# An encoder block on one core: q and k of three heads ahead of every v and gate, all v and gates as groups of seven products

## The chip, the cores and the metric

The kernel runs on one core of a Trainium2 chip. The metric is the device time of one execution in microseconds (us); less is better. Engines are called PE (TensorE: matmuls), DVE (VectorE), ACT (ScalarE), POOL (GpSimd) and SP (SyncE, which issues most transfers).

## The reference

One layer on x of 512 tokens and 1024 features, all in float32. Cut to what the change touches:

```python
h = rmsnorm(x, g_mix)
xc, gb, gc, q, k, v, g_sw, gate_a, gate_r = split(h @ w_in)   # 1024 x5, 2048 x2, 1024 x2 columns
# 4 heads: q, k of 256 columns, v of 512
q, k = rotary(q) * 256 ** -0.5, rotary(k)
ret = forward retention (gamma_f, with the diagonal) + backward retention (gamma_b, strictly future)
y_r = (groupnorm(ret) * silu(g_sw)) @ w_r_out
y_a = (gb * conv3(gc * xc)) @ w_a_out
x = x + (sigmoid(gate_a) * y_a + sigmoid(gate_r) * y_r) @ w_o
x = x + (silu(rms(x) @ w_gate) * (rms(x) @ w_up)) @ w_down
y = rmsnorm(x, g_final)
```

Retention of a head is (q k^T * decay) v, where the decay of a pair of tokens is gamma to the power of their distance.

## The kernel before, in words

Each float32 matrix is split into two parts: `split` rounds it (`hi`, an ACT copy) and takes the rest (`lo`, a DVE difference), and `mm3` does three matmuls for one product (hi hi, hi lo, lo hi). Weights stream from memory in the order of a list, `plan()`: SP loads raw pieces into 10 buffers (`raw`), ACT and DVE split them into 5 units (`whi`, `wlo`), PE uses them in order. The raw loads run four items of the list ahead, the splits two units.

The list has two kinds of items. A chunk is a plain block of weights. A quad is a group of seven products in place of eight (Strassen's way): for four blocks of weights, b11 to b22, DVE adds raw pieces (L244) to make the weight sums t1 to t4, and x has its own sums s1 to s4 (`sums`). `strassen` runs the seven products of 24 matmuls into PSUM and forms the four results with ACT copies (`snap`) and DVE additions (L390, L395, L402).

The beginning goes so:

- SP loads weights, the gains `cols` and x in turn, in pieces of 256 KB (`prefetch_block`, `load_x`). x with its gain is split into `xu`; the row sums of squares (`SumSq`) give 1/rms: `rstd_tokens` lets PE add over the features, takes the power on POOL and writes a diagonal; `rstd_row` lets PE spread it into a row over all partitions (L493, L494).
- v and the swish gate of head 0 are two plain products from `xu` (`token_major`); ACT multiplies the result by 1/rms on its way out of PSUM. Meanwhile DVE multiplies x by the row and splits it again, into `xg`, and makes the sums of x.
- From then on: q and k of head 0 from `xg` (`do_qk`), then for each further head a quad of v and gate and `do_qk`; then two quads of the branch gates. `do_qk` is two chunks of 48 matmuls; DVE rotates the results straight out of PSUM (L619 to L621) and `keep` splits and stores them to memory.
- The decay tables of the four heads (`decays`) need the logarithm of gamma, a series in small DVE steps (`lw`, `lgam`, L506 to L525). A table is one exponential over 896 columns; its store is on SP's queue.

Later stages (gated convolution, scores, outputs, feed-forward) are not touched, but for the last two products: `ev` calls `to_y` (add, square and sum), `put` for the block before (scale and store) and `rms`.

A scheduler sets the order on each engine from the written order, the dependencies and its own model of durations; each engine then works strictly in its order. Short-lived tiles (`t512`) rotate through 9 buffers, large ones (`big`) through 14.

Of the kernel before, what the change touches and what calls it, by code (L numbers as in the profile page):

```python
# [46 lines left out]


# [7 lines left out]
def plan():  # L56
# [86 lines left out]
def block_kernel(ctx: ExitStack, tc: tile.TileContext, xT, xtok, wpack, wquad, cols, decs, rot, g_ffn, g_final, out):  # L143
# [24 lines left out]
    def split(src, hi, lo, scale=None):  # L168

        if scale is None:  # L170
            nc.scalar.copy(hi, src)  # L171
            nc.vector.tensor_tensor(out=lo, in0=src, in1=hi.bitcast(F32), op=ALU.subtract)  # L172
        else:
            nc.scalar.activation(hi, src, AF.Copy, scale=scale)  # L174
            nc.vector.scalar_tensor_tensor(  # L175
                out=lo, in0=src, scalar=scale, in1=hi.bitcast(F32),
                op0=ALU.mult, op1=ALU.subtract)

# [10 lines left out]
    block = [0]  # L189
    ready = []  # L190
# [9 lines left out]
    def prefetch_block(pieces, loads, splits, inbig):  # L200
# [6 lines left out]
        for c in range(2 * per):  # L207
            nc.sync.dma_start(st[c // per][:, c % per * m:(c % per + 1) * m], wpack[i][:, c * m:(c + 1) * m])
            if loads:
                loads(c)  # L210
        for half in range(2):
            hi, lo = unit(inbig)
            units.append((hi, lo))
            for c in range(per):
                sl = slice(c * m, (c + 1) * m)
                split(st[half][:, sl], hi[:, sl], lo[:, sl])
# [191 lines left out]

    ones = const.tile([P, P], F32, name="ones")
# [6 lines left out]
    cols_sb = const.tile([P, N_COLS], F32, name="cols_sb")  # L416
# [12 lines left out]
    def load_x(k, n=1):  # L429
        if k == 0:  # L430
            nc.sync.dma_start(cols_sb, cols)
        nc.sync.dma_start(xs[k // 4][:, k % 4:k % 4 + n, :], xT[:, k:k + n, :])
# [11 lines left out]
    prefetch(2)  # L444
# [6 lines left out]
    class SumSq:  # L451
# [18 lines left out]
        def rstd_tokens(self):  # L470
# [17 lines left out]
            return r  # L488
# [9 lines left out]
    for k in range(8):  # L498
        ss.add(xs[k // 4][:, k % 4, :])
    ss.split()  # L500

# [25 lines left out]

    def decays():
        delta_i = big.tile([P, 896], mybir.dt.int32, tag="big", name="delta_i", padded_shape=[P, 2048])
        nc.gpsimd.iota(delta_i, pattern=[[1, 896]], base=-384, channel_multiplier=-1)  # L530
        delta = big.tile([P, 896], F32, tag="big", name="delta", padded_shape=[P, 2048])
        nc.vector.tensor_copy(delta, delta_i)
        for h in range(HEADS):
            scr = big.tile([P, 896], F32, tag="big", name="scr", padded_shape=[P, 2048])
            tab = misctile(896, "tab")
# [681 lines left out]
```

## Time and profile before

| | |
|---|---|
| Runs | 1043.32, 1044.6, 1044.88 us; median 1044.6 |
| Profiled execution | 1043.97 us, span 1042.2 us |
| PE | 1028.3 us busy |
| DVE, ACT, POOL | 875.5, 523.4, 107.7 us busy |
| From memory, to memory | 135.56 MB, 38.54 MB |
| Granted PE clock | 0.998 |

A row of the timeline is: start in us, duration, engine, line of the kernel, operation, output<-input, shapes, count, and in brackets how long the engine stood before and for whom. A row of the list of waits is: who waited <- for whom: us in total, times, longest. A row of the chain of work is: start, duration, what. Matmuls overlap, so the pace is read from the starts.

### The profile page before, as it was taken

To read this page: it belongs to the slowest core of one execution; us is meant where nothing else is said; L and a number is where in the kernel's file an instruction comes from. 1 tells how busy PE (TensorE), PEld (TensorE's weight loads), DVE (VectorE), ACT (ScalarE), POOL (GpSimd) and SP (SyncE) were. 2 spreads that over 40 slices of the span, in tenths; PEclk is the share of its full clock that TensorE was granted. 3 is DMA by queue.
4 is the path that set the end of the run, shared out by engine and by line. 5 is a ranking of instruction groups with operands and counts; after the bars stand their busy time and mean duration, and the time that the engine had idled before them with its cause. 6 is when DMAs were issued, how large, how long until landed. Compare 5 with 4: busy or idle time off the path is not lost.

```text
span 1042.2 us, 14832 instructions
## 1 busy us (share of the span) xinstructions
PE 1028.3 (99%) x5664; PEld 897.0 (86%) x5664; DVE 875.5 (84%) x1127; ACT 523.4 (50%) x698; POOL 107.7 (10%) x180
## 2 busy tenths in 40 slices
PE   8999999999999999999999999999999999999996
PEld 7788888888888998888888888889998999899985
DVE  6999786858787888697989998669998899889995
ACT  6546745452656545243443234355555565556553
POOL 0121111111111004202011000000002000110011
PEclk9999999999999999999999999999999999999999
DMA  9635638173645576919176535630319322663322
GB/s 325 223 117 201 236 123 281 71 254 119 199 141 182 169 284 233 341 42 358 42 283 247 205 111 173 236 113 28 92 45 275 117 85 78 193 152 102 122 35 87
DMA packets 49688, 175.07 MB, mean 168 GB/s; under 512 B 6480, under 2 KB 6480, under 8 KB 46288
## 3 DMA queue, kind: packets, MB, share of 16 engines
q1 hardware_dynamic: 36592, 131.12, 36.9%
q0 software_dynamic: 13024, 43.00, 12.9%
q8 instruction: 44, 0.72, 0.3%
q14 instruction: 28, 0.23, 0.1%
HBM read 135.56 MB, written 38.54 MB: 167 GB/s over the span
## 4 chain that ended last, share of the span: by engine, by line
PE 77%; issue 9%; DVE 7%; DMA 3%; POOL 2%; ACT 1%; SPq 0%; POOLq 0%; DVEq 0%; ACTq 0%
PE bank L369 29%; PE bank L325 27%; PE bank L285 7%; PE bank L284 7%; PE bank L286 7%; DVE wlo L172 1%; POOL z L566 1%; DVE big L185 1%; DMA big<-ql 1%; DMA big<-xT 1%; DMA z<-t 1%; DMA tab<-tab 0%; DVE big L172 0%; DVE t L464 0%; DVE big L175 0%
## 5 line engine op out<-in xcount | busy, mean ns | idle before, releaser
L171 ACT CAST whi<-raw 128x1024 fp32r<-128x1024 f32 (+1 forms) x281 | 288.6, 1032 | 302.7 <-PE bank L369 66.4
L172 DVE TENSOR_TENSOR wlo<-raw,whi 128x1024 fp32r<-128x1024 f32 (+1 forms) x281 | 335.8, 1202 | 108.8 <-ACT whi L171 107.8
L325 PE MATMUL bank<-xform,whi 128*128 128x256 f32 x1440 | 260.3, 283 | 0.0
L325 PEld LDWEIGHTS bank<-xform,whi 128*128 128x128 f32 x1440 | 224.8, 192 | 0.7 <-ACT t L376 0.6
L325 PE MATMUL bank<-xform,wlo 128*128 128x256 f32 x720 | 203.7, 283 | 0.0
L369 PE MATMUL bank<-whi,big 128*128 128x512 f32 x548 | 172.4, 390 | 0.0
L244 DVE TENSOR_TENSOR raw<-raw 128x1024 f32<-128x1024 f32 (+1 forms) x124 | 148.5, 1205 | 1.8 <-DMA raw<-wquad 0.4
L325 PEld LDWEIGHTS bank<-xform,wlo 128*128 128x128 f32 x720 | 138.2, 192 | 0.0
L369 PEld LDWEIGHTS bank<-whi,big 128*128 128x128 f32 x548 | 102.7, 188 | 22.4 <-DVE big L172 0.6
L369 PE MATMUL bank<-wlo,big 128*128 128x512 f32 x274 | 106.7, 389 | 0.0
L369 PE MATMUL bank<-whi,xform 128*128 128x512 f32 x320 | 101.2, 389 | 0.3 <-ACT t L376 0.3
L284 PE MATMUL bank<-whi,big 128*128 128x512 f32 x240 | 94.3, 395 | 1.8 <-ACT big L174 1.8
L285 PE MATMUL bank<-wlo,big 128*128 128x512 f32 x240 | 94.3, 393 | 0.0
L286 PE MATMUL bank<-whi,big 128*128 128x512 f32 x240 | 93.4, 392 | 0.0
L284 PE MATMUL bank<-big,whi 128*128 128x512 f32 x224 | 87.1, 389 | 0.0
L285 PE MATMUL bank<-big,whi 128*128 128x512 f32 x224 | 87.1, 389 | 0.0
L286 PE MATMUL bank<-big,wlo 128*128 128x512 f32 x224 | 87.1, 389 | 0.0
L376 ACT COPY t<-bank 128x512 f32<-128x512 f32 x96 | 55.5, 585 | 35.8 <-PE bank L369 17.2
L369 PEld LDWEIGHTS bank<-whi,xform 128*128 128x128 f32 x320 | 60.1, 188 | 13.1 <-ACT t L376 0.7
L369 PE MATMUL bank<-wlo,xform 128*128 128x512 f32 x160 | 62.2, 389 | 0.0
L369 PEld LDWEIGHTS bank<-wlo,big 128*128 128x128 f32 x274 | 51.4, 188 | 10.5
L284 PEld LDWEIGHTS bank<-whi,big 128*128 128x128 f32 x240 | 45.5, 190 | 12.5 <-ACT big L174 2.1
(173 smaller groups left out, 1398.6 us busy)
## 6 DMA issues: line engine op xcount, KB each, us to landing
raw<-wquad SPq DMA_DIRECT2D x124, 512.0 KB, 4.4
raw<-wpack SPq DMA_DIRECT2D x58, 512.0 KB, 4.9
z<-t POOLq DMA_DIRECT2D x24, 256.0 KB, 4.9
zform<-z POOLq DMA_DIRECT2D x6, 1024.0 KB, 6.2
v<-t POOLq DMA_DIRECT2D x16, 256.0 KB, 5.0
sg<-t POOLq DMA_DIRECT2D x16, 256.0 KB, 3.3
qh<-t POOLq DMA_DIRECT2D x16, 256.0 KB, 2.6
ql<-t POOLq DMA_DIRECT2D x16, 256.0 KB, 2.7
```

What stands on the lines that cost most here:

```text
L171: nc.scalar.copy(hi, src)
L172: nc.vector.tensor_tensor(out=lo, in0=src, in1=hi.bitcast(F32), op=ALU.subtract)
L185: nc.vector.transpose(o[:, :, :, b, :], i[:, :, :, q, :])
L244: nc.vector.tensor_tensor(out=t, in0=t, in1=raws[quad, more, u][:, 0:n], op=ALU.add)
L284: nc.tensor.matmul(ps, lh, rh, start=first, stop=False)
L285: nc.tensor.matmul(ps, lh, rl, start=False, stop=False)
L286: nc.tensor.matmul(ps, ll, rh, start=False, stop=last)
L325: nc.tensor.matmul(o, l[:, c], r[:, k], start=start and s == 0 and k == 0 and i == 0, stop=stop and k == 3 and i == 2, skip_group_check=True)
L369: nc.tensor.matmul(pss[tt], l, r[:, c], start=start and k == 0 and i == 0, stop=stop and k == n - 1 and i == 2, skip_group_check=True)
L376: nc.scalar.copy(t, ps)
L566: nc.gpsimd.dma_start(dst, t)
```

## The change

- The list begins with six chunks that hold q and k of heads 0, 1 and 2 side by side (256 + 256 columns). They are multiplied by `xu`, without 1/rms, into four banks at a time, and ACT copies the banks to large tiles (`early`). Their rotation comes later, one q or k at a time, at the sixth product of each of six quads (`turn_one`), with a rotation table that has been multiplied by the row (`rcn`).
- v and gate of head 0 become a quad like the others; only head 3 still runs `do_qk`.
- x is multiplied by the row and split, and the sums are made, within those chunks; the small steps for the logarithms follow. `decays` works on 512 columns twice: two exponentials (forward and backward) per head, and one product over the 128 columns where both count; stores are on POOL's queue, ahead of the first quad.
- At the start x goes ahead of weights; x and weights come in pieces of 256, 256 and 512 KB; `cols` is loaded on ACT's queue; the first weights are rounded by DVE.
- Order is written down in three places (`issue_after`): x splits after the first weight split, squares after weight splits, and at the end `put` after the addition and the square of the next block.

```diff
+EARLY = 3
-    for c in (C_V, C_G):
+    for h in range(EARLY):
         for r in (0, 512):
-            b("w_in", r, 4, c, 512)
+            b("w_in", r, 4, (C_Q + h * QK, C_K + h * QK), 512)
     for h in range(HEADS):
-        if h:
-            quad(C_V + h * VD, C_G + h * VD)
-        a("w_in", C_Q + h * QK)
-        a("w_in", C_K + h * QK)
+        quad(C_V + h * VD, C_G + h * VD)
+        if h >= EARLY:
+            a("w_in", C_Q + h * QK)
+            a("w_in", C_K + h * QK)
...
-        for c in range(2 * per):
-            nc.sync.dma_start(st[c // per][:, c % per * m:(c % per + 1) * m], wpack[i][:, c * m:(c + 1) * m])
+        for c, (o, n) in enumerate(((0, 512), (512, 512), (QH, QH)) if pieces > 2 else ((0, QH), (QH, QH))):
             if loads:
                 loads(c)
+            nc.sync.dma_start(st[o // QH][:, o % QH:o % QH + n], wpack[i][:, o:o + n])
...
+                round = None if made else nc.vector.tensor_copy
+                made.append(split(st[half][:, sl], hi[:, sl], lo[:, sl], round=round))
...
+    nc.scalar.dma_start(cols_sb, cols)
...
-    prefetch(4, load_x, split_x)
-    for k in (4, 6):
-        load_x(k, 2)
-    for k in range(4, 8):
+    def split_two(k):
         split_x(k)
+        split_x(k + 1)
+    def split_next(k):
+        with tc.issue_after(made[0].ins):
+            split_x(k)
+    prefetch(4, lambda c: load_x(c, 1 + c // 2), split_next)
+    prefetch(2, lambda c: load_x(4 + 2 * c, 2), lambda c: split_two(4 + 2 * c))
...
+        with tc.issue_after(made[min(k + 1, 3)].ins):
+            ss.add(xs[k // 4][:, k % 4, :])
...
+    def decays():
+        d = []
+        for base, op in ((0, ALU.max), (-384, ALU.min)):
+            delta = t512(mybir.dt.int32)
+            nc.gpsimd.iota(delta, pattern=[[1, 512]], base=base, channel_multiplier=-1)
+            d.append(t512())
+            nc.vector.tensor_scalar(out=d[-1], in0=delta, scalar1=0.0, scalar2=None, op0=op)
+        for h in range(HEADS):
+            f, g = t512(), t512()
+            nc.scalar.activation(f, d[0], AF.Exp, scale=lgam[:, h:h + 1])
+            nc.scalar.activation(g, d[1], AF.Exp, scale=lgam[:, 4 + h:5 + h])
+            nc.vector.tensor_tensor(out=f[:, 0:P], in0=f[:, 0:P], in1=g[:, 384:512], op=ALU.mult)
+            store(tabs[h][:, 0:384], g[:, 0:384])
+            store(tabs[h][:, 384:896], f)
...
+    for h in range(EARLY):
+        pss = [bank() for _ in range(4)]
+        for kk in range(8):
+            if kk % 4 == 0:
+                c = Chunk()
+            if (h, kk) == (0, 7):
+                ss.rstd_tokens()
+            if (h, kk) == (1, 1):
+                rrow = snap(ss.rstd_row())
...
+            for m in range(4):
+                mm3(pss[m], c.w(kk % 4, m * P, P), act_pair(xu, kk), kk == 0, kk == 7)
+        t = bigtile()
+        for m in range(4):
+            nc.scalar.copy(t[:, m, :], pss[m])
+        early.append(t)
...
-    for dst, func in ((vd[0], AF.Copy), (sgd[0], AF.Silu)):
...
-        token_major(xu, 0, 2, ev, None if rtok else before_v)
...
+        nc.vector.tensor_tensor(out=rcn[:, i, :], in0=rcs[:, i, :], in1=rrow, op=ALU.mult)
+    held = [(h, j) for h in range(EARLY) for j in range(2)]
+    def turn_one():
+        if held:
+            h, j = held.pop(0)
+            rotate(h, j, early[h][:, 2 * j, :], early[h][:, 2 * j + 1, :], rcn)
...
             store(left[:, 2 + tt, :], t)
+            if tt:
+                turn_one()
...
+    decays()
     for h in range(HEADS):
-        if h:
-            do_quad(vd[h], sgd[h], AF.Silu)
-        do_qk(h)
+        do_quad(vd[h], sgd[h], AF.Silu)
+        if h >= EARLY:
+            do_qk(h)
     for j in range(2):
         do_quad(gad[j], grd[j], AF.Sigmoid, AF.Sigmoid)
-    decays()
...
     def ev(ps, nb, half):
-        to_y(ps, nb, half)
+        add, square = to_y(ps, nb, half)
         if held:
-            put(held.pop())
+            with tc.issue_after(add.ins), tc.issue_after(square.ins):
+                put(held.pop())
```

DVE's order around the diagonal of 1/rms, before. `rtokv` is the mean square per token, `t_372` the diagonal, `lw` the small steps of the logarithms, `wlo` the rest of a weight piece:

```order
L517 TENSOR_TENSOR lw<-lw 128x8
L172 TENSOR_TENSOR wlo<-raw,whi 128x1024
L518 TENSOR_SCALAR lw<-lw 128x8
L479 TENSOR_SCALAR rtokv<-bank 128x4
L517 TENSOR_TENSOR lw<-lw 128x8
L518 TENSOR_SCALAR lw<-lw 128x8
L485 TENSOR_SCALAR t_372<-ident,rtok 128x128
```

And now (`t_337` is the diagonal, `big<-big,cols_sb,t_396` the multiplication of x by the row):

```order
L174 TENSOR_TENSOR wlo<-raw,whi 128x1024
L489 TENSOR_SCALAR rtokv<-bank 128x4
L495 TENSOR_SCALAR t_337<-ident,rtok 128x128 x4
L174 TENSOR_TENSOR wlo<-raw,whi 128x1024
L174 TENSOR_TENSOR t_343<-t_337,t_342 128x512
L174 TENSOR_TENSOR wlo<-raw,whi 128x1024 x2
L570 SCALAR_TENSOR_TENSOR big<-big,cols_sb,t_396 128x512 x8
```

The steps of the logarithms have moved away from the diagonal, to a place behind the multiplication of x. On PE, 24 matmuls now stand between the sums and the row, where 12 stood.

ACT's order ahead of a quad's first products, before (here the end of the plain gate product; `xform<-big` rounds a sum of x, `t_538` to `t_547` are the gate's results):

```order
L171 CAST xform<-big 128x1024
L576 ACT_TABLE_LOAD
L576 ACTIVATE t_538<-bank,rtok 128x512
L171 CAST xform<-big 128x1024
L576 ACTIVATE t_541<-bank,rtok 128x512
L576 ACTIVATE t_544<-bank,rtok 128x512
L576 ACTIVATE t_547<-bank,rtok 128x512
L171 CAST xform<-big 128x1024
L171 CAST whi<-raw 128x1024
L171 CAST xform<-big 128x1024
```

And now, ahead of the first quad (`lgam` are the logarithms, L524 and L525 the exponentials, of which the last two of eight are shown; `big<-bank` copies a bank of q or k of head 2; the last row rounds the second half of the second product's weights):

```order
L524 ACTIVATE t_733<-t_706,lgam 128x512
L525 ACTIVATE t_734<-t_710,lgam 128x512
L579 COPY big<-bank 128x512 x2
L173 CAST xform<-big 128x1024
L579 COPY big<-bank 128x512 x2
L173 CAST xform<-big 128x1024 x3
L173 CAST whi<-raw 128x1024
```

The exponentials and the copies of the last chunk's banks stand ahead of the casts of the sums of x, and those ahead of a weight piece of the first quad.

DVE's order at the very end, before (L1087 adds a PSUM bank to y, L1097 prepares the root, L1111 scales a finished block):

```order
L1111 SCALAR_TENSOR_TENSOR big<-big,fin,gf 128x512 x2
L1087 TENSOR_TENSOR big<-bank,big 128x512
L1097 SCALAR_TENSOR_TENSOR fin<-fin 128x1
L1111 SCALAR_TENSOR_TENSOR big<-big,fin,gf 128x512
L1087 TENSOR_TENSOR big<-bank,big 128x512
L1097 SCALAR_TENSOR_TENSOR fin<-fin 128x1
L1111 SCALAR_TENSOR_TENSOR big<-big,fin,gf 128x512
```

And now, with the same three kinds at L1122, L1133 and L1147:

```order
L1122 TENSOR_TENSOR big<-bank,big 128x512
L1147 SCALAR_TENSOR_TENSOR big<-big,fin,gf 128x512 x2
L1133 SCALAR_TENSOR_TENSOR fin<-fin 128x1
L1122 TENSOR_TENSOR big<-bank,big 128x512
L1147 SCALAR_TENSOR_TENSOR big<-big,fin,gf 128x512
L1133 SCALAR_TENSOR_TENSOR fin<-fin 128x1
L1147 SCALAR_TENSOR_TENSOR big<-big,fin,gf 128x512
```

The scaling of a block now stands behind the next block's addition, not ahead of it.

More of the change, by code (lines that the diff above doesn't have):

```diff
@@ L189, in block_kernel @@
     block = [0]
+    made = []
     ready = []
@@ L503, in block_kernel @@
+    xf = sums(*(xs[i][:, :, o:o + 256] for o in (0, 256) for i in range(2)))
+    for n, i, o in (("a11", 0, 0), ("a12", 1, 0), ("a22", 1, 256)):
+        xf[n] = tuple(t[i][:, :, o:o + 256] for t in xg)
+    xforms = {n: of(t) for n, t in xf.items()}
     dec = const.tile([P, 8], F32, name="dec")
```

146 lines of the change are left out of this document (61 added, 85 removed).

## The prediction

> **What bounds the kernel now.** I read the page's busy times first, then the list of what TensorE (PE) waits for, then the chain of work in order of time, and last the timeline of the places where PE stands.
>
> ```profile
> span 1042.2 us, 14832 instructions
> PE 1028.3 (99%) x5664; PEld 897.0 (86%) x5664; DVE 875.5 (84%) x1127; ACT 523.4 (50%) x698; POOL 107.7 (10%) x180
> ...
> PE bank L284 <- ACT big L174: 1.8, 1, 1.8
> PE bank L493 <- ACT t L171: 1.7, 1, 1.7
> ...
> 198.26 38.08 PE bank L369 x168
> ```
>
> PE is busy for 1028.3 of 1042.2 us, and the two longest waits of its list are 1.8 and 1.7 us. So the time is the number of matmuls times their pace, plus 13.9 us at the start, at one wait in the beginning and at the end. The pace is in the third row: 168 matmuls of 512 columns, one whole group of seven products, take 38.08 us, 0.2267 us each (the 0.39 us that the page gives for one is its length; they overlap). Only two kinds of things can move the time: fewer matmuls, or less standing. And one thing can spoil it: VectorE (DVE) is 84% busy, and a busier DVE could make PE wait for weights.
>
> **Fewer matmuls.** Before, v and the gate of head 0 are two plain products of 8 x 4 x 3 = 96 matmuls each, 192 together. Now they are a group of seven products of 24 matmuls, 168. Queries and keys of heads 0 to 2 keep 96 matmuls a head, only with all four output blocks side by side. 24 matmuls x 0.2267 us = **-5.4 us**, all on PE's path. This term has no unknown price.
>
> **The wait before the row of 1/rms.** PE multiplies the row sums by ones, DVE, GpSimd (POOL) and ScalarE (ACT) make the reciprocal roots and their diagonal, and PE spreads that into a row (L493).
>
> ```profile
> 28.47 0.25 PE L476 MATMUL bank<-ones_r,t 128*128 128x2 f32 x1
> 28.61 0.17 DVE L518 TENSOR_SCALAR lw<-lw 128x8 f32<-128x8 f32 x1
> 28.81 0.17 DVE L517 TENSOR_TENSOR lw<-lw 128x8 f32<-128x8 f32 x1
> 28.90 1.22 DVE L172 TENSOR_TENSOR wlo<-raw,whi 128x1024 fp32r<-128x1024 f32 x1
> 30.11 0.15 DVE L479 TENSOR_SCALAR rtokv<-bank 128x4 f32<-128x4 f32 x1
> 30.41 1.02 POOL L482 TENSOR_TENSOR rtok<-rtokv,mhalf 128x4 f32<-128x4 f32 x1 [5.75 <-DVE lw L517]
> 31.21 0.39 PE L286 MATMUL bank<-whi,big 128*128 128x512 f32 x1
> 32.66 0.62 ACT L171 CAST t<-t 128x512 fp32r<-128x512 f32 x1 [6.03 <-DVE lw L518]
> 33.33 0.50 PE L493 MATMUL bank<-t,ones_r 128*128 128x512 f32 x1 [1.72 <-ACT t L171]
> ```
>
> The chain from 28.47 to 33.33 is 4.9 us long; PE has 12 matmuls (2.7 us) to do meanwhile, and its issue stands from 31.21 + 0.23 = 31.44 to 33.33, 1.9 us. Now the order has 24 matmuls there, 5.4 us, and the small steps of the decay's logarithm (lw), which lay between, come later. Ahead of the diagonal's cast on ACT there are now a copy out of PSUM (0.6 us) and one weight cast (1.05 us), which fit into the 3.0 us that DVE and POOL need up to there (28.47 to 32.66, less the 1.2 us of a weight difference that DVE did first). I take **-1.9 us**; the ends are -2.1 (with the small gap in front of L494 gone too) and -0.9 (if a weight difference of 1.2 us stands before the diagonal once more).
>
> **The start.**
>
> ```profile
> 0.73 0.39 SPq L208 DMA_DIRECT2D raw<-wpack  x1
> ...
> 1.64 0.42 SPq L432 DMA_DIRECT2D big<-xT  x1
> ...
> 4.18 0.62 ACT L171 CAST whi<-raw 128x512 fp32r<-128x512 f32 x1 [1.86 <-DMA raw<-wpack]
> ...
> 5.90 0.72 ACT L174 ACTIVATE big<-big,cols_sb 128x512 fp32r<-128x512 f32 x1 [1.10 <-DMA big<-xT]
> ...
> 6.67 0.79 PE L284 MATMUL bank<-whi,big 128*128 128x512 f32 x1 [1.85 <-ACT big L174]
> ...
> 7.32 0.42 DVE L462 COPY t<-t 128x512 f32<-128x512 f32 x1
> ...
> 9.82 0.63 PE L285 MATMUL bank<-wlo,big 128*128 128x512 f32 x1
> 10.25 0.48 PE L286 MATMUL bank<-whi,big 128*128 128x512 f32 x1
> 10.57 0.39 PE L284 MATMUL bank<-whi,big 128*128 128x512 f32 x1
> ```
>
> The first transfer lands 3.45 us after its issue, the third (the first piece of x) 4.26 us after, and x then passes ACT. Now x is first: it lands at 4.18, and ACT is done at 4.90. The weights are second, issued at 1.18, since the gains go by ACT's own queue; they land between 1.18 + 3.45 = 4.63 and 1.18 + 4.26 = 5.44, and DVE rounds them in 0.42 us like the copy shown. The first matmul starts between 5.05 and 5.86 in place of 6.67. I take 5.6, **-1.1 us**, near the later end, because two transfers share the engines by then. Nothing hides this time: PE has no other work there, and all later work moves up with it. Against it stands the pace: before 10.25 one matmul follows another in 0.43 us, after it in 0.23 us and less. If the fast pace begins as many us after the first matmul as now (3.6), the whole 1.1 us is won.
> [...]
> The larger pieces of x and weights (512 KB) come later as a whole than their first halves did. PE needs the third piece after 24 matmuls, at about 12.5; I put nothing there, with 0.7 us as the bad end.
>
> **The end.**
>
> ```profile
> 1033.33 0.39 PE L369 MATMUL bank<-whi,big 128*128 128x512 f32 x1
> 1034.79 0.75 DVE L1111 SCALAR_TENSOR_TENSOR big<-big,fin,gf 128x512 f32<-128x512 f32 x1 [0.65 <-POOL fin L1099]
> 1035.46 0.68 DVE L1087 TENSOR_TENSOR big<-bank,big 128x512 f32<-128x512 f32 x1
> 1036.18 0.63 ACT L1089 ACTIVATE t<-big 128x512 f32<-128x512 f32 x1 [0.67 <-DVE big L1087]
> 1036.93 0.16 DVE L1097 SCALAR_TENSOR_TENSOR fin<-fin 128x1 f32<-128x1 f32 x1 [0.79 <-ACT t L1089]
> 1037.75 0.75 DVE L1111 SCALAR_TENSOR_TENSOR big<-big,fin,gf 128x512 f32<-128x512 f32 x1 [0.66 <-POOL fin L1099]
> ```
>
> The last matmul ends at 1033.72, but the addition that takes it (L1087) starts at 1035.46: in DVE's order the scaling of the block before (L1111) stands ahead of it and waits for POOL until 1034.79. Now the addition is ordered first. It can start at about 1033.9, and the scaling moved behind it (0.67 us) fits into the 1.47 us between the addition's start and L1097, which waits for ACT. The rest of the chain is the same: **-1.5 us**, ends -1.6 and -0.8 (if the scaling, now behind, delays L1097).
>
> **What DVE has to bear.** Six rotations of held q and k now lie inside groups of seven products, one half head in each; before they lay beside the plain products of q and k.
>
> ```profile
> 71.51 0.68 DVE L619 TENSOR_TENSOR t<-bank,rcs 128x512 f32<-128x512 f32 x1
> 72.11 0.68 DVE L620 TENSOR_TENSOR t<-bank,rcs 128x512 f32<-128x512 f32 x1
> 72.71 1.22 DVE L244 TENSOR_TENSOR raw<-raw 128x1024 f32<-128x1024 f32 x1
> 73.84 0.69 DVE L621 TENSOR_TENSOR t<-t,t 128x512 f32<-128x512 f32 x1
> ...
> 296.20:334.30 38.10, 38.10 (x171) 31.55 (x170) 27.80 (x27) 21.66 (x28) 4.32 (x8) 1.00 0.51 166
> ...
> 500.00:600.00 100.00, 99.57 (x439) 82.16 (x438) 93.68 (x140) 37.34 (x51) 9.34 (x17) 1.00 0.55 205
> ...
> 800.00:900.00 100.00, 100.00 (x754) 96.29 (x753) 94.30 (x112) 56.81 (x75) 1.75 (x2) 1.00 0.36 110
> ```
>
> In the windows the columns are PE, PE's weight loads, DVE, ACT, POOL. From start to start an operation on 512 columns costs 0.60 us and one on 1024 costs 1.13. A group of seven products alone has 27.8 us of DVE work in 38.1 us. Half a head's rotation is 2 x (3 operations and one difference) = 8 x 0.60 = 4.8 us. Together 32.6 us, 86%: under the 93.7% and 94.3% at which PE lost 0.4 us and nothing in the last two rows. So the load alone costs nothing.
> Its order can. Between a group's start and the first difference that its third product needs, DVE now has 7 short and 5 long operations, 4.2 + 5.7 = 9.9 us; the PE comes to that product after 48 matmuls, 10.9 us. The cover is 1 us, at each of five such places.
>
> ```profile
> v<-t POOLq DMA_DIRECT2D x16, 256.0 KB, 5.0
> ...
> L171 ACT CAST whi<-raw 128x1024 fp32r<-128x1024 f32 x28 | 29.3, 1048 | 20.7 <-PE bank L369 13.2 <-DVE raw L244 2.7 <-issue 2.5
> ...
> L376 ACT COPY t<-bank 128x512 f32<-128x512 f32 x96 | 55.5, 585 | 35.8 <-PE bank L369 17.2
> ...
> 36.15 3.81 SPq L232 DMA_DIRECT2D raw<-wquad  x2
> ```
>
> A rotation's second half also reuses buffers that stores of v have just left. They are issued some 4 us ahead of the group's end (24 matmuls, 5.4 us, less a copy of 0.6 and the issue) and take 5.0 us, so they land about 1 us into the next group, when DVE is still at the rows before.
> The first group is the tightest place. Call its start on PE T (about 74 us). The buffer of the second product's first weights comes free 48 matmuls before, at T - 10.9; cast, difference, eight lw steps (0.2 us each) and one sum later the logarithms are known, at T - 5.8. On ACT then stand in a row 8 exponentials and 4 copies (0.6 each), 4 casts of the sums of x and a weight cast (1.05 each): 12.4 us, to T + 6.6, and the difference behind it ends at T + 7.9. PE wants it after 36 matmuls, at T + 8.2. I take **+0.6 us** for this place and the five others together; the ends are 0 and 2, with no gain possible since PE already runs through there.
>
> **Edits that I cost at nothing.** The decay tables: 13 long DVE operations before, 6 short ones now; PE waits for none. Their stores move from SP's queue, where they stood between weight loads that landed in time, to POOL's, which is 10% busy. The twelve copies of held banks (7 us of ACT, spread over three heads) and two products of the rotation table with the row (1.2 us of DVE) lie beside 65 us of plain products. Six fewer table loads on ACT help nobody who waits.
>
> **Sum.** -5.4 - 1.9 - 1.1 - 1.5 + 0.6 = **-9.3 us** against the profiled execution's 1043.97 us (span 1042.2 and 1.8 around it): 1034.7. The median of the runs shown, 1044.6, is 0.6 higher, so 1035.3.
>
> **Rivals.**
> *DVE's order binds.* If the cover of 1 us at each group's start is not there, PE stands 0.5 to 1 us at five places and 2 us at the first group: 4.5 to 7 us in place of 0.6, 1039.2 to 1041.7. For it: DVE waits for ACT's casts in order, and the cover is thin. Against it: the 94.3% row without a PE wait.
> *ACT's queue at the first group (slower).* The 8 exponentials stand ahead of the copies that free PSUM and of the casts of x, and wait for the logarithms, whose input load now stands on SP's queue behind two weight loads. Each us that it is late beyond 0.3 us stops PE as long. It ends slower than before by over 0.2% once it is 9.9 + 2.1, about 12 us late, logarithms at T + 6.5: 1047 and more. Against it: of these two loads the second belongs to the row at 36.15, and both loads of that row are issued by 40, over 30 us before T.
> [...]
> *Better.* No stall at all and a start at 5.05: 1034.1, or 1032.8 in a run as fast as the fastest shown.
>
> **How the numbers follow.** The forecast holds with 0.74 (1032.5 to 1038.5); DVE's order 0.13; the late start 0.06, inside that span; ACT's queue in small (under 12 us) 0.03, in full 0.04. A measurement of this kernel tells about 0.2%, 2.1 us, from no change. Faster by more than that: the forecast, the late start, DVE's order and a part of the rest, 0.92; within it 0.04; slower 0.04. The range from 1032.5 to 1040.0 takes in the first half of DVE's order and leaves out some 0.15.
>
> **What would show it.** PE's matmuls in the trace fall by 24; L502 (the row) is issued without a wait; the first real matmul starts between 5.0 and 5.9; the last addition starts within 0.3 us of the last matmul. In the windows of the first six groups PE stays at 100% with DVE near 86%. I am wrong if PE's list shows waits for ACT or DVE inside those groups, most of all within 10 us of the first one's start.

## The result and the profile after

| | before | changed |
|---|---|---|
| Runs side by side | 1044.11 us median (1043.32 to 1044.88, 4 runs) | 1031.76 us median (1031.33 to 1033.17, 4 runs) |
| Ratio, 95% interval | | 0.9887 [0.9875, 0.9900] |
| Profiled execution | 1043.97 us, span 1042.2 | 1033.17 us, span 1031.4 |
| All runs of both, over all experiments | 1043.59 us median (1041.57 to 1046.12, 56 runs) | 1032.84 us median (1031.26 to 1034.63, 17 runs) |

The change makes the kernel 1.1% faster. The forecast was 1035.3 us with a range of 1032.5 to 1040.0, so the direction was right and the gain too small: the result lies 3.5 us under the forecast and 0.7 us under the range. The median over all 17 runs, 1032.84 us, would lie just inside it. One execution, of decays_later, took 3205.68 us; it counts as slow and is left out of all comparisons.

The busy times of the changed kernel, and its whole list of waits of PE:

```profile
span 1031.4 us, 14797 instructions
...
PE 1021.8 (99%) x5640; PEld 892.9 (87%) x5640; DVE 886.6 (86%) x1143; ACT 529.5 (51%) x717; POOL 114.9 (11%) x189
...
PE bank L424 <- DVE lw L609: 1.0, 1, 1.0
PE bank L291 <- DVE whi L173: 0.9, 1, 0.9
PE bank L376 <- DVE wlo L174: 0.4, 1, 0.4
PE bank L376 <- ACT t L383: 0.2, 1, 0.2
```

PE has 24 matmuls fewer (5664 to 5640). The two long waits of before, for x at the start (1.8) and for the diagonal of 1/rms (1.7), have left the list. The first row is the warm-up, which waits for a constant. What stands now is 0.9 us for the first weights, 0.4 us at the first group of seven products, and 0.2 us at 781 us. Four places of the changed timeline answer to those of the prediction: the first matmul, the row of 1/rms (L502, L503), the first group, and the end.

```profile
4.15 0.72 ACT L176 ACTIVATE big<-big,cols_sb 128x512 fp32r<-128x512 f32 x1 [1.40 <-DMA cols_sb<-cols]
5.15 0.43 DVE L173 CAST whi<-raw 128x512 fp32r<-128x512 f32 x1 [4.14 <-DMA raw<-wpack]
5.72 1.62 PE L291 MATMUL bank<-big,whi 128*128 128x512 f32 x3 [0.89 <-DVE whi L173]
...
32.85 0.40 PE L293 MATMUL bank<-big,wlo 128*128 128x512 f32 x1
33.09 0.39 PE L502 MATMUL bank<-t,ones_r 128*128 128x512 f32 x1
33.32 0.40 PE L503 MATMUL bank<-t,ones_r 128*128 128x512 f32 x1
...
80.38 1.06 ACT L173 CAST whi<-raw 128x1024 fp32r<-128x1024 f32 x1
82.04 1.22 DVE L174 TENSOR_TENSOR wlo<-raw,whi 128x1024 fp32r<-128x1024 f32 x1
83.31 0.50 PE L376 MATMUL bank<-wlo,xform 128*128 128x512 f32 x1 [0.37 <-DVE wlo L174]
...
1023.88 0.39 PE L376 MATMUL bank<-whi,big 128*128 128x512 f32 x1
1024.30 0.69 DVE L1122 TENSOR_TENSOR big<-bank,big 128x512 f32<-128x512 f32 x1 [0.64 <-PE bank L376]
1024.91 0.74 DVE L1147 SCALAR_TENSOR_TENSOR big<-big,fin,gf 128x512 f32<-128x512 f32 x1
1025.78 0.16 DVE L1133 SCALAR_TENSOR_TENSOR fin<-fin 128x1 f32<-128x1 f32 x1
```

x and the weights arrive in the order that the prediction worked out (ACT done at 4.87, DVE at 5.58), and the first matmul starts at 5.72 in place of 6.67. The row of 1/rms follows the matmul before it by 0.24 us: no wait. At the first group, which PE begins at 74.39, the third product's weight cast runs on ACT only at 80.38, the difference ends at 83.26, and PE stands for it. At the end the addition starts 0.03 us after the last matmul's end, and the scaling behind it is over before L1133.

To see where the 10.8 us of the profiled pair went, I walked through all starts of matmuls and took as lost whatever exceeds the pace of 0.2267 us per 512 columns. A loss is thus a wait together with the small gap behind it. Two losses of before are not in the prediction's sum at all. These are their rows before, the first with the work on DVE and ACT that delays it, the second with the loads on SP's queue:

```profile
144.98 1.22 DVE L172 TENSOR_TENSOR wlo<-raw,whi 128x1024 fp32r<-128x1024 f32 x1
146.11 0.69 DVE L621 TENSOR_TENSOR t<-t,t 128x512 f32<-128x512 f32 x1
146.88 0.62 ACT L171 CAST t<-t 128x512 fp32r<-128x512 f32 x1 [2.15 <-issue]
147.41 1.04 ACT L171 CAST whi<-raw 128x1024 fp32r<-128x1024 f32 x1
148.35 1.07 ACT L376 COPY t<-bank 128x512 f32<-128x512 f32 x2
148.99 0.50 PE L369 MATMUL bank<-whi,xform 128*128 128x512 f32 x1 [0.30 <-ACT t L376]
...
521.90 0.96 SPq L728 DMA_DIRECT2D big<-qh  x1
523.03 0.33 SPq L728 DMA_DIRECT2D big<-ql  x1
532.10 0.50 PE L285 MATMUL bank<-big 128*128 128x512 f32 x1 [0.43 <-DMA big<-ql]
```

At 146 us a rotation (L621) stands on DVE behind a weight difference; ACT's cast of the rotated half waits for it, and the copies that free PSUM for the group stand behind that cast. This was the old place of a rotation, between the plain products of q and k and the next group. Whether that place alone made the loss is taken up in experiment 5. At 532 us the first scores wait for q's second part, whose load was issued late, since the load ahead of it held SP for 0.96 us. In the changed kernel the same two loads take 0.33 and 0.42 us:

```profile
512.60 0.33 SPq L763 DMA_DIRECT2D big<-qh  x1
512.98 0.42 SPq L763 DMA_DIRECT2D big<-ql  x1
```

Both losses are gone in the changed kernel. I profiled before three times and the changed kernel four times in all, and give the terms for the first pair and as means:

| term, us | predicted | first pair | mean, 3 and 4 profiles |
|---|---|---|---|
| 24 matmuls | -5.4 | -5.44 | -5.44 |
| wait at the row (before: 2.3, 2.2, 1.5 lost) | -1.9 | -2.3 | -2.0 |
| first matmul (mean 6.84 to 5.73) | -1.1 | -0.95 | -1.1 |
| last matmul's start to span's end (mean 8.84 to 7.53) | -1.5 | -1.3 | -1.3 |
| stall at the first group (after: 0.65, 0, 0, 0) | +0.6 | +0.65 | +0.2 |
| near 148 us (before: 0.56, 0.19, 0.27) | none | -0.56 | -0.3 |
| near 531 us (before: 0.70, 1.18, 0.71) | none | -0.70 | -0.9 |
| sum | -9.3 | -10.6 | -10.8 |
| measured spans | | -10.8 | -11.1 |

### The profile page after: what moved, and what is told of

The parts are those of the page before. It is cut to its first block, busy times and chain, and to the rows that moved or that the text cites. A ratio compares the mean times of both kernels' runs of the same rounds, so it can differ in the third digit from the quotient of the medians.

```text
span 1031.4 us, 14797 instructions
## 1 busy us (share of the span) xinstructions
PE 1021.8 (99%) x5640; PEld 892.9 (87%) x5640; DVE 886.6 (86%) x1143; ACT 529.5 (51%) x717; POOL 114.9 (11%) x189
## 4 chain that ended last, share of the span: by engine, by line
PE 96%; DVE 2%; DMA 1%; issue 1%; ACT 0%; POOLq 0%; POOL 0%; SPq 0%
PE bank L376 34%; PE bank L332 27%; PE bank L291 11%; PE bank L292 11%; PE bank L293 11%; DMA raw<-wquad 1%; DVE wlo L174 1%; DMA raw<-wpack 0%; PE bank L945 0%; PE bank L896 0%; DVE xform L174 0%; DVE big L174 0%; DVE big L1147 0%; DVE t L998 0%; DVE t L1014 0%
## 5 line engine op out<-in xcount | busy, mean ns | idle before, releaser
L174 DVE TENSOR_TENSOR wlo<-raw,whi 128x1024 fp32r<-128x1024 f32 (+1 forms) x287 | 340.2, 1199 | 82.2 <-ACT whi L173 81.1
L376 PE MATMUL bank<-whi,big 128*128 128x512 f32 x596 | 187.5, 390 | 0.2 <-ACT t L383 0.2
L251 DVE TENSOR_TENSOR raw<-raw 128x1024 f32<-128x1024 f32 (+1 forms) x132 | 156.9, 1202 | 3.0 <-DMA raw<-wquad 1.8
L376 PEld LDWEIGHTS bank<-whi,big 128*128 128x128 f32 x596 | 111.7, 188 | 24.3 <-ACT t L383 0.6
L376 PE MATMUL bank<-whi,xform 128*128 128x512 f32 x384 | 121.2, 389 | 0.0
L376 PE MATMUL bank<-wlo,big 128*128 128x512 f32 x298 | 116.0, 389 | 0.0
L376 PEld LDWEIGHTS bank<-whi,xform 128*128 128x128 f32 x384 | 72.1, 188 | 15.0
L376 PE MATMUL bank<-wlo,xform 128*128 128x512 f32 x192 | 74.8, 390 | 0.4 <-DVE wlo L174 0.4
L291 PE MATMUL bank<-whi,big 128*128 128x512 f32 x176 | 68.9, 392 | 0.0
L292 PE MATMUL bank<-wlo,big 128*128 128x512 f32 x176 | 68.5, 389 | 0.0
L293 PE MATMUL bank<-whi,big 128*128 128x512 f32 x176 | 68.1, 390 | 0.0
L376 PEld LDWEIGHTS bank<-wlo,big 128*128 128x128 f32 x298 | 56.0, 188 | 11.5
L291 PEld LDWEIGHTS bank<-big,whi 128*128 128x128 f32 x224 | 42.5, 190 | 9.9 <-ACT big L176 1.2
```

The costliest lines, as they stand in the source:

```text
L251: nc.vector.tensor_tensor(out=t, in0=t, in1=raws[quad, more, u][:, 0:n], op=ALU.add)
L291: nc.tensor.matmul(ps, lh, rh, start=first, stop=False)
L292: nc.tensor.matmul(ps, lh, rl, start=False, stop=False)
L293: nc.tensor.matmul(ps, ll, rh, start=False, stop=last)
L376: nc.tensor.matmul(pss[tt], l, r[:, c], start=start and k == 0 and i == 0, stop=stop and k == n - 1 and i == 2, skip_group_check=True)
```

## The experiments

The runs of before that an experiment is compared with were made on the same chip in the same session. Several kernels differ by 1 to 2 us only, which is near the scatter of single executions, so the profiles carry most verdicts.

**1. The changed kernel again (after_again, after_third, after_fourth).** No edit.

> The changed kernel once more, for more runs and a second profile. Theory A (the terms read from the two traces are all: 24 matmuls -5.4, the row -2.3, the start -0.95, the end -1.35, two middle waits -0.56 and -0.70, the first group +0.65, small ones -0.1, together -10.8): the ratio comes to 0.9885 to 0.9900, and the second profile has the same waits as the first, 0.5 us at the first group and none in the middle. Rival B (runs without a profile win more, some 12 us, by the clock at the start): ratio 0.9875 to 0.9885, and executions 1 to 2 us apart whose traces differ in when the fast pace begins.

> The changed kernel once more, beside the three below on the same chip. Theory A (the change's gain is 5.4 for the matmuls, 2.3 for the row, 1.0 for the start, 1.4 for the end and about 1.2 for two waits in the middle of the kernel before, and the rest is scatter from where the fast pace begins): ratio 0.988 to 0.990. Rival B (the first result was a lucky chip): 0.991 or more. Profile: TensorE loses nothing between 140 and 160 us nor between 510 and 540 us; the pace doubles at 9 to 11 us, or early, before 8.

> The changed kernel once more. Ratio 0.988 to 0.990. In its profile no loss of TensorE over 0.2 us between 100 and 700 us; at the first group's third product 0 or about 0.6 us lost (both have been seen). The fast pace begins between 6 and 10.5 us, and the profile's own time lies 1 to 2 us lower when it begins before 7.

Ratios 0.9898 [0.9884, 0.9911], 0.9889 [0.9872, 0.9907] and 0.9897 [0.9884, 0.9910]; medians 1032.88, 1032.04 and 1033.03 us. The gain repeats. In none of the three profiles did PE lose over 0.2 us between 36 and 700 us, so the stall at the first group is not in every execution, and the half of Theory A in after_again that expected it again was wrong. Its origin can be read from the start of the exponentials, first in the changed kernel's first profile, then in after_again:

```profile
69.76 0.72 ACT L524 ACTIVATE t<-t,lgam 128x512 f32<-128x512 f32 x1 [4.88 <-DVE lgam L624]
...
68.65 0.72 ACT L524 ACTIVATE t<-t,lgam 128x512 f32<-128x512 f32 x1 [3.65 <-DVE lgam L624]
```

With the stall the logarithms (`lgam`) were known 4.7 us before the group's first matmul; in the three profiles without it, 5.9 us before. Down ACT's row of exponentials, copies and casts this moves the end of the difference from 7.6 to 8.9 us after the group's start, and PE wants it at 8.2. The profile of warm2 (experiment 8) has the late logarithms and the same stall; undo_start (experiment 4) has late ones too, but another order of casts on ACT, and no stall. Why the logarithms came 1.2 us later in some executions is open.

The fast pace began at 10.0 us, with the first matmuls, and at 10.2 us. The execution in which it was there at once took 1031.40 us, the least of its five; the two others took 1032.84 and 1032.85. These are the first rows of after_third, to set beside the 5.72 and the three slow matmuls in 1.42 us of the changed kernel:

```profile
5.84 0.93 PE L291 MATMUL bank<-big,whi 128*128 128x512 f32 x3 [1.14 <-DVE whi L173]
6.61 0.86 PE L292 MATMUL bank<-big,whi 128*128 128x512 f32 x3
```

Here three matmuls take 0.77 us. By the 60th matmul that saves 1.4 us against the profile of the first pair, and it shows how far single executions of one kernel can lie apart.

**2. The kernel before again (before_again, before_third).** No edit.

> The kernel before, profiled a second time. Theory A (the sum lacked two waits in the middle): TensorE stands again near 148 us (for the copy of a bank, 0.56 us lost in all) and near 531 us (for the later scores' input, 0.70 us), and 2.3 us in front of the row of 1/rms. Rival B (those two waits belong to one execution): one or both are under 0.2 us this time, and then they explain nothing of the median. Both: the first real matmul at 6.5 to 6.8; the pace doubles anywhere from 7 to 11 us.

> The kernel before once more. Theory A: 0.2 to 1.0 us lost near 148 us, 0 to 1.3 us near 531 us, together 0.8 to 1.5; 2.1 to 2.4 us lost at the row. Rival B: both middle waits absent.

1043.60 and 1042.98 us. The losses near 148 us were 0.19 and 0.27, those near 531 us 1.18 and 0.71. Theory A holds in both for the second place; the first is a small one whose size varies, and in before_again it is under the bound that I had set for B. At the row they lost 2.2 and 1.5 us; the 1.5 is under the 2.1 to 2.4 that was expected.

**3. The end undone (undo_tail), and the end alone (before_tail).**

```diff
-            with tc.issue_after(add.ins), tc.issue_after(square.ins):
-                put(held.pop())
+            put(held.pop())
```

> The changed kernel with the end as before (the scaling of a block is ordered by the scheduler again). Theory A: 1.35 us slower than the changed kernel, the last addition starts 1.5 us after the last matmul ends in place of 0.05. Rival (the end is hidden by the last stores of y): no difference. Below 0.5 us the rival holds.

> The kernel before with the change's order at the end alone (scaling of a finished block behind the next block's addition). Theory A: 1.35 to 1.7 us faster than before, ratio about 0.9986; the time from the last matmul to the span's end falls from 8.9 us to 7.2 to 7.6. Rival B (the scaling, now behind, delays the preparation of the root): 0.8 us or less. The interval of the runs may be as wide as the effect, so the profile's tail decides.

undo_tail: 1032.73 us, 0.9900 [0.9887, 0.9914], not to be told from after_again by time; by the bound set beforehand (0.5 us) the rival would hold. The profiles speak against it. From the last matmul's start to the end it takes 9.2 us against 7.5 in after_again, and what hides this in the profiled execution is the start: the fast pace was there with the first matmuls, so that PE reached its 60th matmul 1.8 us earlier than in after_again. Whether the same holds for the three executions that were only timed is not known. The addition again stands behind a scaling that waits for POOL:

```profile
1021.46 0.39 PE L376 MATMUL bank<-whi,big 128*128 128x512 f32 x1
1022.92 0.75 DVE L1147 SCALAR_TENSOR_TENSOR big<-big,fin,gf 128x512 f32<-128x512 f32 x1 [0.65 <-POOL fin L1135]
1023.59 0.68 DVE L1122 TENSOR_TENSOR big<-bank,big 128x512 f32<-128x512 f32 x1
```

before_tail: 1041.50 us, 0.9986 [0.9977, 0.9995], 1.8 us under before, and 7.3 us from the last matmul (1032.10) to the end of its span (1039.4), where before takes 8.8. The end is worth 1.3 to 1.7 us in the profiles, as A had it.

**4. The start undone (undo_start).** x and weights in the old order and pieces, the gains on SP's queue, the first weights rounded by ACT.

```diff
-        for c, (o, n) in enumerate(((0, 512), (512, 512), (QH, QH)) if pieces > 2 else ((0, QH), (QH, QH))):
+        for c in range(2 * per):
...
-                round = None if made else nc.vector.tensor_copy
+                round = None
...
-    nc.scalar.dma_start(cols_sb, cols)
...
-    prefetch(4, lambda c: load_x(c, 1 + c // 2), split_next)
-    prefetch(2, lambda c: load_x(4 + 2 * c, 2), lambda c: split_two(4 + 2 * c))
+    prefetch(4, load_x, split_x)
```

> The changed kernel with the start as before (weights first, pieces of 256 KB, the gains on SP's queue, the first weights rounded by ScalarE, order by the scheduler). Theory A: first real matmul at 6.6 us, the fast pace 3.9 us after it, 0.95 us slower than the changed kernel. Rival (the fast pace begins at a time of its own): 0.4 us slower. Second rival (the smaller pieces leave a wait at the second chunk, as the trace of before had 0.1 us): 1.1 us and more.

1033.42 us, 0.9909 [0.9893, 0.9924]. The first matmul is back at 6.67, and two more waits for splits of x and weights come up at 9.55 and 19.09, 1.27 us lost. In the trace the second rival is nearest: with q and k first the old start costs 2.2 us, not 1.0. By time it is 0.5 us (1033.42 against 1032.88), near the first rival. The profiled execution shows less because its fast pace was there at once, from 7.0 us; for the others this isn't known, so the price of the old start is not settled by time.

**5. The tables of the decay later (decays_later), and their new form in the kernel before (before_decays).** In the first, `decays()` moves from ahead of the first group to behind it:

```diff
-    decays()
...
+        if h == 0:
+            decays()
```

In the second, before gets the new function (two powers of 512 columns, stores on POOL) at its old place in the code.

> The changed kernel with the decay tables written after the first group of seven products and not ahead of it, so that the exponentials do not stand ahead of the copies and casts on ScalarE. Theory A (they cause the 0.5 to 0.65 us that TensorE stood at the first group): that wait is gone, 0.6 us faster than the changed kernel. Rival (the copies of the last banks and the casts alone make ScalarE late there): the wait stays, no difference. Third case: the exponentials disturb a later group, 0 to 1 us slower, with a wait there.

> The kernel before with the change's form of the decay tables (two powers of 512 columns, stores on POOL's queue) at their old place. Theory A: the wait of VectorE for a table's buffer (5.1 us in two waits before) is gone, and so is TensorE's at about 148 us (0.56 us lost); 0.5 to 0.6 us faster. Rival B: the wait at 148 is of another origin and stays, no difference. Third case: eight exponentials on ScalarE stand ahead of copies out of PSUM as they did in the run with the tables later, and TensorE stands 2 us or more there: slower by 2 to 7 us.

Both are bad: 1039.85 us, 0.9962 [0.9949, 0.9976], which is 7 us slower than after_again and far beyond the third case, and 1048.66 us, 1.0047 [1.0035, 1.0059], 5 us slower than before. The rows of decays_later show why:

```profile
121.28 1.28 ACT L524 ACT_TABLE_LOAD   x1
122.57 0.72 ACT L524 ACTIVATE t<-t,lgam 128x512 f32<-128x512 f32 x1
...
126.88 0.70 ACT L525 ACTIVATE t<-t,lgam 128x512 f32<-128x512 f32 x1
127.49 1.04 ACT L383 COPY t<-bank 128x512 f32<-128x512 f32 x2
128.11 0.80 PE L376 MATMUL bank<-whi,xform 128*128 128x512 f32 x1 [3.96 <-ACT t L383]
128.70 0.63 PE L376 MATMUL bank<-wlo,xform 128*128 128x512 f32 x1
129.12 1.06 PE L376 MATMUL bank<-whi,xform 128*128 128x512 f32 x2
```

A table load and eight exponentials, 6.2 us in one piece, stand on ACT ahead of the copies that free PSUM. PE stands 4.1 us, and then runs at half pace (0.42 us from start to start) until 133.7, which costs another 2.7. In before_decays the scheduler put the exponentials at 331 to 342 us, and the same thing happened in the products there: 3.0 us of standing and 2.0 of half pace. So this is the mechanism of the prediction's rival "ACT's queue at the first group" at another place. Where the change has the tables, the eight exponentials stand ahead of copies too, but beside products that don't need those copies at once: in the first profile they run from 69.76 to 74.8 us without a wait of PE. The wait at the first group is absent in decays_later, but it is absent in three of four profiles of the changed kernel too, so this run does not decide its question.

The loss near 148 us is gone in before_decays, as its Theory A had it, and yet a rotation stands at the same place there:

```profile
145.09 0.68 DVE L620 TENSOR_TENSOR t<-t,t 128x512 f32<-128x512 f32 x1
...
147.79 1.07 ACT L376 COPY t<-bank 128x512 f32<-128x512 f32 x2
```

So the rotation's place does not always make the loss. In before the tables are made between 64 and 126 us, and DVE's waits for their buffers (5.1 us) end at 111 and 121. PE lost nothing there, but from 127 us to the rotation at 146 DVE stood only 0.7 us in all, so that a delay at the last table can reach the rotation. That before_decays has no loss speaks for the tables, but PE also comes to this product 0.8 us later there (149.36 us, against 148.53 in before if it had not waited). Which of the two made the loss, the rotation's place or the tables ahead of it, is open; the change removes both.

**6. The logarithm's steps behind the row, in the kernel before (before_row).** The block from `dec` to `lgam` moves behind the sums of x; 12 matmuls stay ahead of the row.

> The kernel before with the small steps of the logarithms moved behind the row of 1/rms; 12 matmuls stand between the sums and the row as before. Theory A (the wait was 4.9 us of chain against 2.7 us of matmuls, and the small steps lay in the chain for part of it): the loss at the row falls from 2.3 us to 0.8 to 1.6. Rival B (the steps cost nothing, the weight difference and POOL's power set the chain): 2.0 us or more stay. Third case (the chain was all the steps'): under 0.4 us stays. In time 0.7 to 1.5 us, nothing, or 2 us faster than before.

The row's loss falls from 2.3 us to 0.5, PE waits 0.18 us there:

```profile
31.76 0.50 PE L493 MATMUL bank<-t,ones_r 128*128 128x512 f32 x1 [0.18 <-ACT t L171]
...
104.62 0.95 ACT L516 ACTIVATE tab<-scr 128x896 f32<-128x896 f32 x1 [1.60 <-DVE scr L515]
105.48 0.57 ACT L376 COPY t<-bank 128x512 f32<-128x512 f32 x1
106.10 0.50 PE L369 MATMUL bank<-whi,big 128*128 128x512 f32 x1 [0.98 <-ACT t L376]
```

So the order of the small steps was most of the wait, a little more than A had allowed, and by this profile the 12 added matmuls of the change would not have been needed for it. But the time is 1044.62 us, 1.0013 [1.0000, 1.0026]: nothing won. The tables, now later, put an exponential that waits for DVE ahead of a copy at 104 us, and PE lost 1.7 us at 87 and 106 us together. The wait had only moved. The profiles of the changed kernel show no loss at these places; the tables' old form, with a chain between DVE and ACT, is gone there.

**7. The group of seven for head 0 undone (undo_quad).** All as changed, but v and gate of head 0 are two plain products, from x that is already multiplied by the row.

```diff
+        if h:
             quad(C_V + h * VD, C_G + h * VD)
+        else:
+            for c in (C_V, C_G):
+                for r in (0, 512):
+                    b("w_in", r, 4, c, 512)
...
+                token_major(xg, 0, 2, ev)
```

> The changed kernel, but v and gate of head 0 as two plain products of 96 matmuls each, from x that is already multiplied by the row; all else as changed. Theory A (the 24 matmuls give their full price and nothing beside it): 5.0 to 5.9 us slower than the changed kernel beside it, ratio to the kernel before about 0.994; no wait of TensorE at the row, none in the middle. Rival B (the group of seven brings waits of its own at the first group, on average 0.6 us or more, so the term is worth less): 4.0 to 4.9 us slower. Third case (the exponentials ahead of the copies stop TensorE here, as in the runs with the tables elsewhere): 8 us slower or more.

1037.65 us, 0.9942 [0.9930, 0.9955], against 1033.03 for after_fourth: 4.6 us. By that figure B would be right; by the interval A is not excluded. The profiles decide for A on the matmuls, and against its "none in the middle". Their spans differ by 4.5 us (1035.4 and 1030.9), but the fast pace began at once in this one and at 10.2 us in the other, a difference of 1.85: 6.35 us are left. Of these 5.44 are the 24 matmuls and 0.98, with the small gap behind it, is the wait for q, which is back:

```profile
515.99 1.42 SPq L778 DMA_DIRECT2D big<-qh  x1
517.45 0.43 SPq L778 DMA_DIRECT2D big<-ql  x1
526.73 0.50 PE L297 MATMUL bank<-big 128*128 128x512 f32 x1 [0.71 <-DMA big<-ql]
```

The load that SP issues in 0.33 us in every profile of a kernel with the group for head 0 took 0.71 to 1.42 in six of the seven without it, and in the seventh (before_tail) the next load took 0.70. With the two plain products the list holds other loads ahead of this one. Why an issue then takes longer is not shown. Nor does a longer issue always cost PE something: five of the seven lost 0.7 to 1.2 us at this place, before_tail and before_decays nothing. Of the ten with the group, nine lost nothing and warm10 0.2.

**8. The warm-up (warm2, warm10, warm12).** Before the first real matmul PE runs 8 products of ones, from 1.04 to 4.8 us. These kernels run 2, 10 or 12.

```diff
-WARM = 8
+WARM = 12
```

> 2 warm-up products, which end at 2.0 us, and then nothing until the first real matmul at 5.6. [...] Third case (the early warm-up matters in no way and costs something): 0.3 us faster or more.

> The changed kernel with 10 warm-up products in place of 8, so that TensorE runs from 1.04 us until the first real matmul without the gap of 0.8 us. [...]

> 12 warm-up products: they end at 6.7 us at the slow pace, which delays the first real matmul by up to 1.1 us when the pace hasn't doubled by then. [...]

2: 1035.01 us, 0.9910 [0.9894, 0.9926]; 10: 1032.18, 0.9887 [0.9869, 0.9905]; 12: 1032.26, 0.9888 [0.9870, 0.9906]; beside them 8 (after_third): 1032.04. More warm-up brings nothing that can be measured. In the profile of 10 the weights arrived later (first matmul at 6.41 us), so that a gap of 0.7 us stayed and the fast pace began only at 10.0. In that of 12 there was no gap and the pace was fast from about 6.5 (1031.43 us, the least of its four). But the medians do not follow, and these runs do not show what sets the start of the fast pace. With 2 products the median is 3.0 us higher, where the third case had 0.3 us less or better. Its profile, the fastest of its five executions, has a span of 1031.3 us against 1029.4 beside it: 0.9 of that is the start, with a fast pace that begins only at about 8.5, and 1.1 are two small waits, at the first group and at 873 us. What held up the slower executions is open. None of the three is faster than the changed kernel by more than the scatter.

## Why the prediction was wrong, point by point

The mechanism of the terms in the sum held. The step that failed is the sixth point, a gain that was put at nothing; a base that was too high, and some luck, did the rest.

- **24 matmuls.** Right: -5.4, measured -5.44, and undo_quad gives it back.
- **The row of 1/rms.** Right in size over three profiles (-2.0 for -1.9). The first profile of before held 2.3, a little over the end of -2.1. Of its two reasons one would have done: in the profile of before_row moving the small steps alone takes most of the wait away (2.3 to 0.5).
- **The start.** Right: 5.72 for 5.6. The fast pace came to stay 3.9 to 4.9 us after the first real matmul in the three profiles of before, and from at once to 4.4 us after it in the four of the changed kernel. So the prediction's condition (3.6 us after it, as it read before) did not hold in every execution, but the slow phase cost nearly the same, 1.6 us as a mean after and 1.8 before. With so few profiles and such scatter it is not shown what sets the start of the fast pace.
- **The end.** Right: -1.3 for -1.5; before_tail, which has this edit alone, shows it.
- **What DVE has to bear.** A little low in load (86% predicted). The stall at the first group came with 0.65 us in one profile of four, at the third product and by the chain that was written down. With the group's start at T, the logarithms were to be known at T - 5.8, the difference to end at T + 7.9; without the stall they came at T - 5.9 and T + 7.6, with it at T - 4.7 and T + 8.9. As a mean it is +0.2, so +0.6 was 0.4 too much. The prediction's own sign of being wrong, a wait for DVE within 10 us of the first group's start, did appear in that one profile, at the price that the sum allowed for it. The other five places cost nothing. The three rows are windows over the first, the second and the last of the six groups; the columns are those of the prediction:

```profile
74.00:112.00 38.00, 37.63 (x166) 30.82 (x165) 29.32 (x30) 26.84 (x35) 5.21 (x10) 1.00 0.53 191
112.00:150.00 38.00, 38.00 (x169) 31.43 (x169) 35.49 (x38) 23.64 (x31) 6.48 (x12) 1.00 0.55 194
...
286.00:324.00 38.00, 38.00 (x169) 31.49 (x168) 33.36 (x36) 22.76 (x30) 6.48 (x12) 1.00 0.54 194
```

DVE is busy for 93% and 88% in the last two, and PE never stands.

- **Edits costed at nothing: the step that failed.** The prediction read the list of PE's waits down to its 1.8 and 1.7, put all of the 13.9 us of standing "at the start, at one wait in the beginning and at the end", and looked only for what the moved work might newly cost. It did not ask what the moved work cost where it had stood. Two further rows of the same list (0.3 us for ACT's copy at 149, 0.4 us for q at 532) were real losses, 1.2 us together as a mean over three profiles with the small gaps after them. Both are gone in all four profiles of the changed kernel. The first lay at a rotation that the change moves, behind tables that it makes in another way and earlier; "PE waits for none", which the prediction says of the tables, is therefore not certain. The second came only beside the two plain products that the change removes, apart from 0.2 us in warm10. That the losses went is shown; what made each of them is argued from rows.
- **The base.** The forecast stood on the median of three runs, 1044.6; over 56 runs before has 1043.59. That is 1.0 of the 3.5 us. About 1.4 are the missing gain (10.75 between the medians of all runs, 9.3 predicted). The last 1.1 is luck: the four runs of the result lie low, all 17 have 1032.84.
- **The rivals.** "DVE's order binds" and the late start, to which the prediction gave 0.06, did not happen: the first matmul came 0.95 us earlier, and PE stood for no later piece of x. "Better" had the right sign, with gains from the wrong places. "ACT's queue" happened at the first group only in small: the 0.65 us in the one profile are its mechanism, logarithms that come late to ACT's row. Two experiments brought a larger case of exponentials ahead of copies about elsewhere, and those kernels were 5 and 7 us slower.

## What to carry to other kernels

When work moves, price both ends: what it may delay where it goes, and which wait it leaves behind where it stood; each small row of the bound engine's list of waits deserves one look at what is queued ahead. A block of exponentials on the engine that also empties PSUM can cost most of its length (here 4.1 of 6.2 us, and a slow stretch behind it) where the bound engine needs that bank next, so place it beside work that does not. A step of 1 us cannot be weighed by a handful of runs that scatter by 3: read it in the trace, in several profiles, and take a base from more than three runs.

## What the runs showed of the hardware that was not expected

A gap in PE's work can cost more than its length (in decays_later 4.1 us of standing and 2.7 us of half pace behind it). At the start of before_again the pace was fast from 7.0 us, and then half from 8.1 to 11.5. The windows of that stretch show the granted clock in the third column from the end:

```profile
7.00:8.00 1.00, 1.00 (x6) 0.83 (x5) 0.69 (x2) 0.71 (x2) 0.00 (x0) 1.00 1.09 262
8.00:9.00 1.00, 1.00 (x4) 0.73 (x3) 0.69 (x1) 0.15 (x1) 0.00 (x0) 0.53 0.94 244
...
10.00:11.00 1.00, 1.00 (x4) 0.81 (x3) 1.00 (x3) 0.86 (x3) 0.00 (x0) 0.50 1.05 414
...
12.00:13.00 1.00, 1.00 (x6) 0.83 (x5) 1.00 (x3) 1.00 (x3) 0.00 (x0) 1.00 1.05 430
```

1.8 us without a matmul (4.8 to 6.6) had come before. In undo_start the same gap (4.8 to 6.7) was followed by no slow stretch. The same slow stretch was seen in the middle of a kernel: at the row in before_decays PE stood 2.3 us, and the next eight matmuls came at 0.43 to 0.48 us each, 1.7 us lost on top. After 3.0 us (before_decays at 340) it was half pace for 3.5 us, after 4.1 us (decays_later) for 5.6 us. After the 1.9 us of standing at the row in before, there was none of it. Slow stretches thus followed gaps of 1.8 to 4.1 us, though not every one, and these runs do not show what decides it. So the wait at the row, which the change takes away, could cost nearly twice its length in some executions (2.3 and 1.7 us in before_decays). The executions that were only timed cannot show how often that happens. The column of the granted clock can't be trusted alone: in before it reads 1.00 from 7 to 10 us, where the matmuls come at 0.43 us, so read the pace from the starts.
